# Layer A of a two-layer trunk: convolution statistics kept in PSUM, four gates kept on chip, a staging pool of its own, and x transposed eight tiles at a time

## The chip, the cores and the metric

The kernel runs on one core of one Trainium2 chip, in one launch. The metric is the device time of that launch in microseconds (us): 1713.63 us before the change, the median of three runs (1712.63 to 1716.33). Five engines work beside each other, each with its own queue in program order: PE (TensorE, matrix products), DVE (VectorE), ACT (ScalarE), POOL (GpSimd) and SP (SyncE, which issues the transfers). Instructions of different engines wait for each other by semaphores.

## The reference

Two layers over a sequence of 1024 tokens with 1024 channels, in float32. Each has one wide input projection, a token mixer, a cross-attention of four heads into 256 memory tokens, a SiLU gate over the whole branch and an output projection; the result is layer-normalized with the residual. In layer A the mixer is a convolution module over 1536 channels:

```python
def conformer_conv(u, conv_w, conv_b, g, b):
    a, gl = jnp.split(u, 2, axis=-1)
    h = a * jax.nn.sigmoid(gl)
    ...                                  # causal depthwise convolution, 31 taps
    return jax.nn.silu(layer_norm(h, g, b))

for i in range(DEPTH):                   # DEPTH = 2: layer A, layer B
    if i % 2 == 0:
        u, qm, gate = split_cols(x @ a_w_in, A_SIZES)
        y_mix = conformer_conv(u, ...)
    else:
        q, k, v, qi, ki, wi, qm, gate = split_cols(x @ b_w_in, B_SIZES)
        y_mix = dsa_attention(...)       # top-256 keys per query, ALiBi
    y_mem = mem_cross_attention(qm, layer_norm(mem), w_mkv)
    y = concatenate([y_mix, y_mem]) * silu(gate)
    x = layer_norm(ALPHA * x + y @ w_out, pg, pb)
```

## The kernel before

**Numbers.** Every fp32 operand of a product is split into a rounded high part and the rest (`hi`, `lo`), and a product is three matmuls (L149, L151, L153 in the input projections; L585, L586, L587 in the output projection). `split_w` loads a piece of weights into `wr`, of which there are three buffers; ScalarE writes the high part `wh` (L131) and POOL the low part `wl` (L132), with six buffers each. So a weight piece can be split when the piece six before it has been used. Activations lie with channels on the partitions, in eight blocks of 128 by 1024 tokens (`xhi`, `xlo`).

**Stages of layer A.** x is loaded and transposed. Twelve blocks of convolution channels follow in pairs, on TensorE as products with the input weights and on VectorE as 31 taps (L433). The sums over channels are gathered on POOL in `sumd` and `sumsq`. Channels 0 to 7 are stored to memory (`d_dram`), channels 8 to 11 stay in the four `co` buffers. Between them stand the four heads of the memory attention (`head_a`) and the twelve gates (`gate_a`: product, SiLU at L325, store to `gate_dram`). Between the gates 2 to 9 stand the keys and values of the memory attention of layer B (`k_b`, `v_b`, called K0, V0 and so on here): eight products of 256 columns, whose result goes through the tile `kvr` (tag `mp`, one buffer, which the softmax of layer A's memory attention uses too) to memory.

**The normalization.** Two products with a matrix of ones (L524, `tot`) sum over the partitions. The mean and 1/std are then written to `sumd` and `sumsq` in SBUF (L530 to L534).

**The output projection.** 16 row blocks of `a_w_out` in four groups of four: first 12 to 15 (memory heads, in `yhi`, `ylo`), then 8 to 11 and 0 to 3 (in `xhi`, `xlo`), then 4 to 7 (again in `yhi`, `ylo`). A group has two column halves with eight token blocks each, so 16 PSUM tiles of twelve matmuls. `WO12.0` is row block 12, column half 0. VectorE adds each tile to `accA` in SBUF, which begins as x (L590, L592). Beside it `conv_y` makes the operand for the next groups: load `dr` (L606), subtract the mean (L611), multiply by 1/std (L612), SiLU on ScalarE (L613), multiply by the gate (L614), split on ScalarE and POOL (L172, L173). After the last group each token block is normalized, transposed four tiles at a time and split for layer B.

**PSUM.** There are eight banks of 128x512. `ps1` holds two for products (`pj`) and two for transposes and scores (`pt`). `psb` has two tiles of two banks (x transposes, two convolution accumulators, `tot`); after the sums are done, `pso` takes its four banks for the output projection.

**Order.** The program is written in the order of the stages; a scheduler with a simulated timeline then sets the order of instructions on each engine, and each engine runs its queue in that order. A pool that is closed frees its space for the next pool, once the last users of its tiles are done.

Of the kernel before, what the change touches and what calls it, by code (L numbers as in the profile page):

```python
# [20 lines left out]
P = 128  # L21
# [43 lines left out]
def trunk(ctx, tc, x, mem, mem_g, mem_b, a_w_in, conv_w, conv_b, ln_g, ln_b,  # L65
# [43 lines left out]
    def psum_t():  # L109
        p, n = banks["pt"]  # L110
        return p.tile([P, 512], F32, tag="pt", bufs=n, name=f"pt{uid()}")
# [95 lines left out]
            nc.vector.scalar_tensor_tensor(dst[:, c], dst[:, c], rs, b[:, c], op0=OP.mult, op1=OP.add)  # L207
            nc.sync.dma_start(o[:, c], dst[:, c])

    def transpose_in(src, hi, lo, t, f=None):  # L210

        for g in range(2):
            o = psum_t()
            for j in range(4):
                k = 4 * g + j
                nc.tensor.transpose(o[:, j * P:(j + 1) * P], src[:, k * P:(k + 1) * P], ident)
            dh, dl = hi[:, 4 * g:4 * g + 4, t * P:(t + 1) * P], lo[:, 4 * g:4 * g + 4, t * P:(t + 1) * P]
            split_ps(dh, dl, o.rearrange("p (a b) -> p a b", a=4))

    def dram(name):  # L220
        return tc.dram_tile([P, T], F32, name=name)

# [2 lines left out]
    with ExitStack() as actx:  # L225
# [4 lines left out]
        def co_tile(name):  # L230
            return convp.tile([P, T], F32, tag="co", bufs=4, name=name)

        hctx = ExitStack()
        hp = hctx.enter_context(pool("hp"))
        c_sh = hp.tile([P, T], F32, name="c_sh")
        psb = hctx.enter_context(pool("psb", side="right", space=PSUM))
        mctx = ExitStack()
        am = mctx.enter_context(pool("am", side="right"))

# [3 lines left out]
        def x_load(t):  # L243
            nc.sync.dma_start(xn[t], x[t * P:(t + 1) * P, :])

        def x_in(t):
            o = psb.tile([P, T], F32, tag="acc", bufs=2, name=f"px{t}")
            for k in range(KD):
                nc.tensor.transpose(o[:, k * P:(k + 1) * P], xn[t][:, k * P:(k + 1) * P], ident)
            split_ps(xhi[:, :, t * P:(t + 1) * P], xlo[:, :, t * P:(t + 1) * P], o.rearrange("p (a b) -> p a b", a=KD))  # L250

        rows = [am.tile([NR, n], F32, tag="sg", bufs=2, name=f"rows{i}") for i, n in enumerate((T, 512))]

        def rows_load():
            nc.gpsimd.memset(rows[1][32:, :], 0.0)
# [18 lines left out]
        def mem_prep():  # L274
            mn = []
            for t in range(2):
                mt = am.tile([P, T], F32, tag="sg", bufs=2, name=f"mt{t}")
# [187 lines left out]
        def head_a(h):  # L465
            kv = am.tile([P, T], F32R, tag="kv", bufs=1, name=f"kva{h}")
            y = am.tile([P, T], F32, tag="y", bufs=1, name=f"ya{h}")
            mem_k(a_w_mkv, h, kv=kv)
            sg = am.tile([P, T], F32, tag="sg", bufs=2, name=f"msgA{h}")
            silu_gate(am, a_w_in, A_GATE + CONV_CH + h * P, sg)  # L470
# [15 lines left out]
            nc.sync.dma_start(kvb_dram[h][:, :512], kr[h])  # L486

        def gate_a(i):
            sg = am.tile([P, T], F32, tag="sg", bufs=2, name=f"ga{i}")
            silu_gate(am, a_w_in, A_GATE + i * P, sg)  # L490
            nc.sync.dma_start(gate_dram[i], sg)

        def u_conv(i):
            hs = [u_pair(i, start=i == 0), u_pair(i + 1)]
# [16 lines left out]
        u_conv(10)  # L511
        gate_a(1)
        head_a(3)
        for i in range(2, 10):
            gate_a(i)
            ((k_b, v_b)[i % 2])((i - 2) // 2)

        with tc.high_priority(offset=3000):
            tot = []
            for src in (sumd, sumsq):  # L520
                o = psb.tile([P, T], F32, tag="acc", bufs=2, name=f"tot{len(tot)}")
                for hf in range(2):
                    hs = slice(hf * 512, (hf + 1) * 512)
                    nc.tensor.matmul(o[:, hs], ones, src[:, hs], start=True, stop=True)  # L524
                tot.append(o)
            mean_b, rstd_b = sumd, sumsq
            for hf in range(2):
                hs = slice(hf * 512, (hf + 1) * 512)
                sq = hp.tile([P, 512], F32, tag="sig", bufs=2, name=f"meansq{hf}")
                nc.scalar.activation(mean_b[:, hs], tot[0][:, hs], AF.Copy, scale=1.0 / CONV_CH)  # L530
                nc.scalar.activation(sq, mean_b[:, hs], AF.Square)
                nc.vector.scalar_tensor_tensor(sq, tot[1][:, hs], 1.0 / CONV_CH, sq, op0=OP.mult, op1=OP.subtract)
                nc.scalar.activation(rstd_b[:, hs], sq, AF.Sqrt, bias=eps)
                nc.vector.reciprocal(rstd_b[:, hs], rstd_b[:, hs])  # L534
        hctx.close()
        yy = actx.enter_context(pool("yy"))
        yhi = yy.tile([P, 4, T], F32R, name="yhi")
# [12 lines left out]
            (sub or nc.vector).tensor_tensor(dl, raw, dh.bitcast(F32), op=OP.subtract)  # L550

        for h in range(MEM_HEADS):
            load_y(am, "sg", ymem_dram[h], yhi[:, h, :], ylo[:, h, :])
            if h % 2 == 1:
                gate_a(10 + h // 2)
        mctx.close()

        if "A1" in dbg:
            for i in range(NCONV):
# [3 lines left out]
            return  # L563


        octx = ExitStack()
        banks["pj"] = (octx.enter_context(pool("pso", side="right", space=PSUM)), 4)
        ao = octx.enter_context(pool("ao", side="right"))
        acc = [ao.tile([P, T], F32, name=f"accA{t}") for t in range(NB)]

        def out_group(w_out, k0, yh, yl, acc, t_order, first=False, after=None, resident=None):

            held, cur = {}, None
            for (hf, t) in t_order:
                if hf != cur:
                    cur = hf
                    if resident is None or hf not in held:
                        held[hf] = [split_w(w_out[(k0 + k) * P:(k0 + k + 1) * P, hf * 512:(hf + 1) * 512], [P, 512],
                                            resident and resident(hf, k)) for k in range(4)]
                    wts = held[hf]  # L580
                o = psum()
                tsl = slice(t * P, (t + 1) * P)
                for k in range(4):
# [19 lines left out]
        def conv_y(i, dh, dl):  # L603
# [2 lines left out]
                nc.sync.dma_start(d, d_dram[i])  # L606
            else:
                d = conv_out[i]
            gt = ao.tile([P, T], F32, tag="gt", bufs=3, name=f"gt{i}")
            nc.sync.dma_start(gt, gate_dram[i])  # L610
            nc.vector.tensor_tensor(d, d, mean_b, op=OP.subtract)  # L611
            nc.vector.tensor_tensor(d, d, rstd_b, op=OP.mult)  # L612
            nc.scalar.activation(d, d, AF.Silu, bias=chan[:, i, TAPS + 2:TAPS + 3], scale=chan[:, i, TAPS + 1:TAPS + 2])  # L613
# [18 lines left out]
        def finish_a(t, hf):  # L632
# [6 lines left out]
            transpose_in(z, xhi, xlo, t)  # L639
            if "A2" in dbg:  # L640
                nc.sync.dma_start(out[t * P:(t + 1) * P, :], z)

        def keep_a(hf, k):
# [2 lines left out]
                g = ao.tile([P, T], F32R, tag="gt", bufs=3, name=f"wg{n}")  # L646
                return g[:, :512], g[:, 512:]

            def own_place(n):
                return [ao.tile([P, 512], F32R, name=f"w{q}{n}") for q in "hl"]  # L650
            return None if hf == 0 else (own_place if k < 2 else gate_place)

        out_group(a_w_out, ids[0], yh, yl, acc, token_major, after=finish_a, resident=keep_a)
        octx.close()
        banks["pj"] = (ps1, 2)
    if "A2" in dbg:
        return

# [443 lines left out]
    with ExitStack() as octx:  # L1102
# [27 lines left out]
        for gi, k0 in enumerate((12, 0, 4, 8)):  # L1130
# [3 lines left out]
                for j in range(4):  # L1134
                    load_y(bo, "yraw", yb_d[k0 + j], yh[:, j, :], yl[:, j, :], gate_d[k0 + j] if k0 + j in LATE_GATES else None)
            if gi < 3:
                out_group(b_w_out, k0, yh, yl, acc, half_major, first=gi == 0)
            else:
                out_group(b_w_out, k0, yh, yl, acc, token_major, after=finish_b, resident=lambda hf, k: keep_b)


# [26 lines left out]
```

## Time and profile before

| | |
|---|---|
| time, median of 3 runs | 1713.63 us (1712.63 to 1716.33) |
| profiled execution | 1715.64 us, span 1713.6 us |
| mean granted TensorE clock | 0.991 |
| PE busy | 1651.4 us, 96% |
| DVE, ACT, POOL busy | 68%, 44%, 41% |
| layer A | to about 800 us |
| keys and values of layer B, gates 3 to 9 | about 470 to 585 us |
| output projection of layer A | 604 to 800 us, groups from 604, 649, 700 and 751 |

The span runs from the first to the last instruction of the profiled execution; the time of the execution has some 2 us around it. An engine's busy time counts its instructions' durations once where they overlap. In the rows below a time in square brackets is what the engine stood idle before the instruction, with the instruction that released it. Matmuls overlap: a product of 512 columns is listed with 0.39 us, and the next one starts 0.23 us after it.

### The profile page before, as it was taken

To read this page: it belongs to the slowest core of one execution; us is meant where nothing else is said; L and a number is where in the kernel's file an instruction comes from. 1 tells how busy PE (TensorE), PEld (TensorE's weight loads), DVE (VectorE), ACT (ScalarE), POOL (GpSimd) and SP (SyncE) were. 2 spreads that over 40 slices of the span, in tenths; PEclk is the share of its full clock that TensorE was granted. 3 is DMA by queue.
4 is the path that set the end of the run, shared out by engine and by line. 5 is a ranking of instruction groups with operands and counts; after the bars stand their busy time and mean duration, and the time that the engine had idled before them with its cause. 6 is when DMAs were issued, how large, how long until landed. Compare 5 with 4: busy or idle time off the path is not lost.

```text
span 1713.6 us, 22459 instructions
## 1 busy us (share of the span) xinstructions
PE 1651.4 (96%) x8214; PEld 1381.1 (81%) x8214; DVE 1173.3 (68%) x1800; ACT 753.3 (44%) x1412; POOL 694.7 (41%) x591
## 2 busy tenths in 40 slices
PE   7999999999999997999999999799999999999997
PEld 6877888888888876788767877688898888888886
DVE  3799899989996649447158999865555554535337
ACT  4333344444443524124456776354544544543221
POOL 2344554645556346444222332433323332342233
PEclk9999999999999999999999999999999999999999
DMA  5121212222243475123221333212121221246212
GB/s 183 50 58 66 86 53 84 68 68 74 74 130 116 131 282 177 62 81 114 62 65 39 92 93 98 86 38 81 50 64 55 74 68 50 63 149 250 86 44 98
DMA packets 138941, 156.88 MB, mean 92 GB/s; under 512 B 8074, under 2 KB 108426, under 8 KB 138832
## 3 DMA queue, kind: packets, MB, share of 16 engines
q1 hardware_dynamic: 138832, 155.47, 28.4%
q8 instruction: 64, 1.05, 0.3%
q14 instruction: 45, 0.37, 0.1%
HBM read 114.81 MB, written 38.80 MB: 90 GB/s over the span
## 4 chain that ended last, share of the span: by engine, by line
PE 57%; DVE 14%; ACT 4%; issue 3%; DMA 2%; POOL 1%; SPq 0%; DVEq 0%; ACTq 0%; POOLq 0%
PE pj L149 9%; PE pj L151 9%; PE pj L153 9%; PE pj L587 5%; PE pj L585 5%; PE pj L586 5%; DVE junk L829 4%; PE pt L981 2%; DVE xs L788 2%; PE S L951 1%; ACT junka L835 1%; PE S L953 1%; PE S L952 1%; PE pv L993 1%; PE pv L997 1%
## 5 line engine op out<-in xcount | busy, mean ns | idle before, releaser
L149 PE MATMUL pj<-xhi,wh 128*128 128x512 f32 (+2 forms) x1328 | 523.9, 395 | 19.1 <-ACT gB L706 10.8
L132 POOL TENSOR_TENSOR wl<-wr,wh 128x512 fp32r<-128x512 f32 (+1 forms) x260 | 352.5, 1362 | 433.7 <-ACT wh L131 412.6
L151 PE MATMUL pj<-xlo,wh 128*128 128x512 f32 (+2 forms) x1328 | 521.6, 393 | 0.6 <-DVE xlo L169 0.5
L153 PE MATMUL pj<-xhi,wl 128*128 128x512 f32 (+2 forms) x1328 | 522.1, 393 | 0.0
L433 DVE SCALAR_TENSOR_TENSOR acc<-h,chan,acc 128x996 f32<-128x996 f32 (+27 forms) x348 | 418.7, 1265 | 16.1 <-ACT acc L423 14.8
L149 PEld LDWEIGHTS pj<-xhi,wh 128*128 128x128 f32 (+1 forms) x1328 | 250.9, 189 | 73.0 <-ACT gB L706 11.6
L153 PEld LDWEIGHTS pj<-xhi,wl 128*128 128x128 f32 (+1 forms) x1328 | 251.1, 189 | 49.6 <-issue 0.2
L151 PEld LDWEIGHTS pj<-xlo,wh 128*128 128x128 f32 (+1 forms) x1328 | 251.1, 189 | 48.9 <-DVE xlo L169 1.4
L131 ACT ACTIVATE wh<-wr 128x512 fp32r<-128x512 f32 x232 | 144.6, 628 | 296.3 <-PE pj L151 155.2
L585 PE MATMUL pj<-wh,xhi 128*128 128x512 f32 x384 | 149.2, 395 | 11.2 <-DVE accA L592 7.7
L586 PE MATMUL pj<-wl,xhi 128*128 128x512 f32 x384 | 150.0, 393 | 0.0
L587 PE MATMUL pj<-wh,xlo 128*128 128x512 f32 x384 | 148.5, 393 | 0.0
L961 POOL TENSOR_SCALAR t<-t,smB 128x128 f32<-128x128 f32 (+3 forms) x96 | 71.6, 747 | 183.1 <-DVE smB L960 87.5
L956 DVE CUSTOM_DVE_ANT_0 t<-S,xs 128x128 f32<-128x128 f32 (+3 forms) x96 | 70.9, 756 | 72.7 <-PE S L953 49.8
L169 DVE TENSOR_TENSOR pl<-pt,ph 128x512 fp32r<-128x512 f32 (+1 forms) x120 | 69.2, 580 | 59.4 <-ACT ph L168 58.5
L585 PEld LDWEIGHTS pj<-wh,xhi 128*128 128x128 f32 x384 | 72.8, 190 | 29.2 <-DVE accA L592 8.6
L959 ACT ACTIVATE t<-t,mxB 128x128 f32<-128x128 f32 (+3 forms) x96 | 74.1, 774 | 46.3 <-DVE mxB L958 46.0
L168 ACT ACTIVATE ph<-pt 128x512 fp32r<-128x512 f32 (+1 forms) x120 | 60.2, 509 | 77.1 <-PE pt L981 71.1
L835 ACT ACTIVATE junka<-xs,cand 128x896 bf16<-128x896 f32 (+2 forms) x93 | 80.3, 864 | 28.3 <-DVE cand L860 22.9
L829 DVE TENSOR_SCALAR_CACHE_REDUCE junk<-xs,cand 128x1024 bf16<-128x1024 f32 (+2 forms) x93 | 89.9, 967 | 2.2
L587 PEld LDWEIGHTS pj<-wh,xlo 128*128 128x128 f32 x384 | 72.7, 189 | 15.7
L586 PEld LDWEIGHTS pj<-wl,xhi 128*128 128x128 f32 x384 | 72.8, 190 | 15.5
(273 smaller groups left out, 2721.0 us busy)
## 6 DMA issues: line engine op xcount, KB each, us to landing
wr<-in_a_w_in_dram SPq DMA_DIRECT2D x88, 256.0 KB
wr<-in_b_w_in_dram SPq DMA_DIRECT2D x76, 256.0 KB
wr<-in_a_w_out_dram SPq DMA_DIRECT2D x32, 256.0 KB
wr<-in_b_w_out_dram SPq DMA_DIRECT2D x32, 256.0 KB
yraw<-yb SPq DMA_DIRECT2D x16, 512.0 KB
gb<-gB SPq DMA_DIRECT2D x15, 512.0 KB
ga<-ga SPq DMA_DIRECT2D x12, 512.0 KB
gt<-ga SPq DMA_DIRECT2D x12, 512.0 KB
```

The source lines that it names most:

```text
L131: nc.scalar.activation(hi, raw, AF.Copy)
L132: nc.gpsimd.tensor_tensor(lo, raw, hi.bitcast(F32), op=OP.subtract)
L149: nc.tensor.matmul(o, wh, xh, start=(k == 0), stop=False)
L151: nc.tensor.matmul(o, wh, xl, start=False, stop=False)
L153: nc.tensor.matmul(o, wl, xh, start=False, stop=(k == KD - 1))
L433: nc.vector.scalar_tensor_tensor(dst[:, s:], h[:, :T - s], w, acc[:, s:], op0=OP.mult, op1=OP.add)
L585: nc.tensor.matmul(o, yh[:, k, tsl], wh, start=(k == 0), stop=False)
L586: nc.tensor.matmul(o, yh[:, k, tsl], wl, start=False, stop=False)
L587: nc.tensor.matmul(o, yl[:, k, tsl], wh, start=False, stop=(k == 3))
L829: nc.vector.tensor_scalar(j[:, :nk(b)], xs(b), th[:, i:i + 1], None, op0=op, op1=OP.add, accum_out=c[:, i:i + 1])
L835: nc.scalar.activation(j[:, :nk(b)], xs(b), AF.Sign, bias=th[:, i:i + 1], scale=-(2.0 ** 24), accum_out=c[:, i:i + 1])
L959: nc.scalar.activation(t, t, AF.Exp, bias=mx[:, e:e + 1], scale=s, accum_out=sm[:, e:e + 1])
```

## The change

1. *Statistics.* The mean and 1/std stay in the PSUM tiles `tot0` and `tot1`; the square root is taken into an SBUF tile half by half, with the reciprocal written to PSUM. The operations of `conv_y` that use them read one operand from PSUM.
2. *Gates.* Gates 8 to 11 aren't stored and loaded again: 8 and 9 lie in `gt` buffers, 10 and 11 in `sumd` and `sumsq`, which are free by then.
3. *Staging pool.* The tag `sg` (gates, rows, memory outputs) moves from `am` into a pool `sgp` of its own. `am` is then closed after V3, with all four K/V pairs placed at gates 2 to 5, and the pool `ao` with `accA` and `gt` is opened there.
4. *Output projection.* Its PSUM tiles alternate between the `pt` and `pj` banks of `ps1`; `psb` stays open. The x1 transposes write eight tiles into one two-bank tile of `psb`, with one split in place of two. The weights kept for the last group lie in `sg` buffers instead of tiles of their own.

```diff
-        psb = hctx.enter_context(pool("psb", side="right", space=PSUM))
+        pctx = ExitStack()
+        psb = pctx.enter_context(pool("psb", side="right", space=PSUM))
...
+        def transpose_in(src, t):
+            o = psb.tile([P, T], F32, tag="acc", bufs=2, name=f"px{uid()}")
+            for k in range(KD):
+                nc.tensor.transpose(o[:, k * P:(k + 1) * P], src[:, k * P:(k + 1) * P], ident)
+            split_ps(xhi[:, :, t * P:(t + 1) * P], xlo[:, :, t * P:(t + 1) * P], o.rearrange("p (a b) -> p a b", a=KD))
...
+        gate_here = {}
+        def gate_stay(i, g):
+            silu_gate(sgp, a_w_in, A_GATE + i * P, g)
+            gate_here[i] = g
...
-        for i in range(2, 10):
+        for i in range(2, 6):
             gate_a(i)
-            ((k_b, v_b)[i % 2])((i - 2) // 2)
+            k_b(i - 2)
+            v_b(i - 2)
+        mctx.close()
+        octx = ExitStack()
+        ao = octx.enter_context(pool("ao", side="right"))
+        acc = [ao.tile([P, T], F32, name=f"accA{t}") for t in range(NB)]
+        for i in range(6, 8):
+            gate_a(i)
...
-            mean_b, rstd_b = sumd, sumsq
+            mean_b, rstd_b = tot
...
-                nc.scalar.activation(rstd_b[:, hs], sq, AF.Sqrt, bias=eps)
-                nc.vector.reciprocal(rstd_b[:, hs], rstd_b[:, hs])
+                nc.scalar.activation(sq, sq, AF.Sqrt, bias=eps)
+                nc.vector.reciprocal(rstd_b[:, hs], sq)
...
-            load_y(am, "sg", ymem_dram[h], yhi[:, h, :], ylo[:, h, :])
+            load_y(sgp, "sg", ymem_dram[h], yhi[:, h, :], ylo[:, h, :])
             if h % 2 == 1:
-                gate_a(10 + h // 2)
-        mctx.close()
+                i = 8 + h // 2
+                gate_stay(i, ao.tile([P, T], F32, tag="gt", bufs=3, name=f"gt{i}"))
+        gate_stay(10, sumd)
+        gate_stay(11, sumsq)
...
-        octx = ExitStack()
-        banks["pj"] = (octx.enter_context(pool("pso", side="right", space=PSUM)), 4)
-        ao = octx.enter_context(pool("ao", side="right"))
-        acc = [ao.tile([P, T], F32, name=f"accA{t}") for t in range(NB)]
+        turn = [0]
+        def psum_a():
+            turn[0] += 1
+            return (psum_t if turn[0] % 2 else psum)()
...
-                o = psum()
+                o = bank()          # bank=psum_a in layer A, bank=psum in layer B
...
-            gt = ao.tile([P, T], F32, tag="gt", bufs=3, name=f"gt{i}")
-            nc.sync.dma_start(gt, gate_dram[i])
+            gt = gate_here.get(i)
+            if gt is None:
+                gt = ao.tile([P, T], F32, tag="gt", bufs=3, name=f"gt{i}")
+                nc.sync.dma_start(gt, gate_dram[i])
...
-            def own_place(n):
-                return [ao.tile([P, 512], F32R, name=f"w{q}{n}") for q in "hl"]
+            def spare_place(n):
+                g = sgp.tile([P, T], F32R, tag="sg", bufs=2, name=f"ws{n}")
+                return g[:, :512], g[:, 512:]
```

The lines of the changed kernel shift by the edit: L325 becomes L321, L359 becomes L355, L606 becomes L620, L600 becomes L614, L543 becomes L553.

How the instructions move shows at three places. First ScalarE's queue at gates 3 and 4. Before: `ga_3946` is gate 3, `wh_4125` and `wh_4131` are the weights of K1, `wh_4164` and `wh_4170` those of gate 5, `vt_4049` is V0, `mp` the softmax of the last head.

```order
L325 ACTIVATE ga_3946<-pj_3959 128x512
L131 ACTIVATE wh_4125<-wr_4123 128x512
L131 ACTIVATE wh_4131<-wr_4129 128x512
L325 ACTIVATE ga_3946<-pj_3985 128x512
L359 ACT_TABLE_LOAD
L359 ACTIVATE mp_3786,sm_3788<-pt_3789,mx_3787 128x256 x2
L131 ACTIVATE wh_4164<-wr_4162 128x512
L131 ACTIVATE wh_4170<-wr_4168 128x512
L310 ACTIVATE vt_4049<-pj_4024 128x256
L359 ACTIVATE mp_3786,sm_3788<-pt_3790,mx_3787 128x256 x2
```

Now: `ga_3993` is gate 3, `wh_4106` the second weight piece of V1, `wh_4145` and `wh_4151` are the weights of gate 4.

```order
L131 ACTIVATE wh_4106<-wr_4104 128x512
L321 ACTIVATE ga_3993<-pj_4006 128x512
L355 ACT_TABLE_LOAD
L355 ACTIVATE mp_3789,sm_3791<-pt_3792,mx_3790 128x256 x2
L131 ACTIVATE wh_4145<-wr_4143 128x512
L131 ACTIVATE wh_4151<-wr_4149 128x512
L355 ACTIVATE mp_3789,sm_3791<-pt_3793,mx_3790 128x256 x2
L321 ACT_TABLE_LOAD
L321 ACTIVATE ga_3993<-pj_4032 128x512
```

Both halves of gate 3 stood ahead of the first table load (L359); now its second half (`pj_4032`) stands behind two exponentials, the weights of gate 4, two more exponentials and a second table load.

Second SP's queue around the loads of x. Before, to the fifth of the loads: `ga_126` is the store of gate 11, `wr_5201` is `WO8.0`.

```order
L491 DMA ga_126<-ga_4808 128x1024
L122 DMA wr_5201<-in_a_w_out_dram 128x512
L600 DMA accA_4881<-in_x_dram 128x1024
L600 DMA accA_4882<-in_x_dram 128x1024
L600 DMA accA_4883<-in_x_dram 128x1024
L600 DMA accA_4884<-in_x_dram 128x1024
L600 DMA accA_4885<-in_x_dram 128x1024
```

Now, to the third of the loads: `wr_4696` is the second half of the weights of gate 9, `wr_4754` the first half of gate 10, `kvb_133` the store of K3 and V3.

```order
L122 DMA wr_4696<-in_a_w_in_dram 128x4x128
L122 DMA wr_4754<-in_a_w_in_dram 128x4x128
L482 DMA kvb_133<-kvr_4357 128x512
L614 DMA accA_4444<-in_x_dram 128x1024
L614 DMA accA_4445<-in_x_dram 128x1024
L614 DMA accA_4446<-in_x_dram 128x1024
```

All eight loads follow one another as before, but now directly behind the store of V3 and ahead of the second half of the weights of gate 10, in front of all of `a_w_out`.

Third POOL's queue where the second weight group begins. Before: `wl_5216` and `wl_5222` are `WO10.0` and `WO11.0`, `wl_5340` is `WO8.1`, `xlo<-dr` are channels 0, 1 and 2.

```order
L173 TENSOR_TENSOR xlo<-co_3435,xhi 128x1024
L173 TENSOR_TENSOR xlo<-dr_5473,xhi 128x1024
L132 TENSOR_TENSOR wl_5216<-wr_5213,wh_5215 128x512
L132 TENSOR_TENSOR wl_5222<-wr_5219,wh_5221 128x512
L132 TENSOR_TENSOR wl_5340<-wr_5337,wh_5339 128x512
L173 TENSOR_TENSOR xlo<-dr_5483,xhi 128x1024
L173 TENSOR_TENSOR xlo<-dr_5493,xhi 128x1024
```

Now: `dr_5488` is channel 3, `dr_5770` and `dr_5780` are channels 4 and 5, `wl_5201` and `wl_5207` are `WO10.0` and `WO11.0`.

```order
L173 TENSOR_TENSOR xlo<-dr_5488,xhi 128x1024
L173 TENSOR_TENSOR ylo<-dr_5770,yhi 128x1024
L132 TENSOR_TENSOR wl_5201<-wr_5198,wh_5200 128x512
L173 TENSOR_TENSOR ylo<-dr_5780,yhi 128x1024
L132 TENSOR_TENSOR wl_5207<-wr_5204,wh_5206 128x512
L173 TENSOR_TENSOR ylo<-dr_5790,yhi 128x1024
```

The low halves of `WO10.0` and `WO11.0` stood behind channel 0's split; now channels 1 to 4 stand ahead of the one and channel 5 ahead of the other. ScalarE's queue has the same sequence there: `yhi` of channel 4, `WO10.0`, `yhi` of channel 5, `WO11.0`.

## Rows read from the trace of the kernel before

**Rows 1.** The page's shares: busy us (share of the span) x instructions.
```profile
PE 1651.4 (96%) x8214; PEld 1381.1 (81%) x8214; DVE 1173.3 (68%) x1800; ACT 753.3 (44%) x1412; POOL 694.7 (41%) x591
```

**Rows 2.** Stretches of the output projection: from:to length, busy us (instructions), clock, DMA, GB/s.
```profile
604.00:649.30 45.30, 44.08 (x190) 35.42 (x190) 25.32 (x23) 10.07 (x14) 21.97 (x10) 1.00 0.74 267
649.30:700.30 51.00, 40.02 (x159) 31.32 (x158) 47.08 (x36) 21.14 (x23) 38.99 (x16) 0.93 0.46 155
```

**Rows 3.** TensorE's timeline: start, us, instruction, [idle before <- what ended it].
```profile
615.66 0.51 PE L585 MATMUL pj<-wh,yhi 128*128 128x512 f32 x1 [1.22 <-DVE accA L590]
...
653.17 0.49 PE L585 MATMUL pj<-wh,xhi 128*128 128x512 f32 x1 [2.41 <-ACT wh L131]
...
654.37 0.79 PE L585 MATMUL pj<-wh,xhi 128*128 128x512 f32 x1 [0.71 <-DVE accA L590]
...
671.02 0.79 PE L585 MATMUL pj<-wh,xhi 128*128 128x512 f32 x1 [5.33 <-DVE accA L592]
...
689.30 0.50 PE L585 MATMUL pj<-wh,xhi 128*128 128x512 f32 x1 [2.41 <-DVE accA L592]
```

**Rows 4.** Stretches behind the two longest stops of TensorE.
```profile
653.80:657.20 3.40, 2.83 (x7) 2.15 (x7) 3.40 (x3) 1.62 (x4) 3.40 (x2) 0.51 0.13 47
670.90:674.30 3.40, 3.28 (x8) 2.61 (x9) 3.40 (x4) 0.80 (x1) 2.94 (x2) 0.50 0.61 209
```

**Rows 5.** VectorE's timeline in the first two groups.
```profile
614.92 0.69 DVE L590 SCALAR_TENSOR_TENSOR accA<-accA,pj 128x512 f32<-128x512 f32 x1 [9.51 <-DMA accA<-in_x_dram]
...
622.96 0.69 DVE L590 SCALAR_TENSOR_TENSOR accA<-accA,pj 128x512 f32<-128x512 f32 x1 [1.08 <-DMA accA<-in_x_dram]
...
626.73 3.68 DVE L614 TENSOR_TENSOR co<-co,gt 128x1024 f32<-128x1024 f32 x2 [1.70 <-DMA gt<-ga]
...
641.10 1.87 DVE L611 TENSOR_TENSOR dr<-dr,sumd 128x1024 f32<-128x1024 f32 x1 [3.29 <-DMA dr<-d_dram]
...
642.89 0.67 DVE L590 SCALAR_TENSOR_TENSOR accA<-accA,pj 128x512 f32<-128x512 f32 x1
...
643.49 2.82 DVE L612 TENSOR_TENSOR dr<-dr,sumsq 128x1024 f32<-128x1024 f32 x1
...
649.10 1.21 DVE L612 TENSOR_TENSOR dr<-dr,sumsq 128x1024 f32<-128x1024 f32 x1
...
694.41 1.89 DVE L592 TENSOR_TENSOR accA<-pj,accA 128x512 f32<-128x512 f32 x3
```

**Rows 6.** SP's timeline, issues of x and of gates.
```profile
611.47 3.80 SPq L600 DMA_DIRECT2D accA<-in_x_dram  x8
615.37 13.14 SPq L610 DMA_DIRECT2D gt<-ga  x4
```

**Rows 7.** POOL's timeline: one 128x1024 operation alone, weight pieces, one split.
```profile
546.91 2.40 POOL L446 TENSOR_TENSOR co<-co,c_sh 128x1024 f32<-128x1024 f32 x1
...
605.67 2.55 POOL L132 TENSOR_TENSOR wl<-wr,wh 128x512 fp32r<-128x512 f32 x2 [5.99 <-PE pj L587]
...
641.85 3.38 POOL L173 TENSOR_TENSOR xlo<-co,xhi 128x1024 fp32r<-128x1024 f32 x1
```

**Rows 8.** ScalarE's timeline at gate 3, and one split of a channel.
```profile
485.15 0.63 ACT L131 ACTIVATE wh<-wr 128x512 fp32r<-128x512 f32 x1 [2.09 <-PE pj L151]
...
485.69 0.58 ACT L325 ACTIVATE ga<-pj 128x512 f32<-128x512 f32 x1
...
486.29 1.28 ACT L359 ACT_TABLE_LOAD   x1
...
487.58 0.47 ACT L359 ACTIVATE mp<-pt,mx 128x256 f32<-128x256 f32 x1
...
651.55 1.04 ACT L172 ACTIVATE xhi<-dr 128x1024 fp32r<-128x1024 f32 x1
```

**Rows 9.** Waits of TensorE from 485 to 500: total, times, longest.
```profile
PE pj L149 <- ACT ga L325: 1.0, 2, 0.8
PE pj L149 <- ACT vt L310: 0.9, 1, 0.9
```

More of the change, by code (lines that the diff above doesn't have):

```diff
@@ L208, in layer_norm_late @@
             nc.sync.dma_start(o[:, c], dst[:, c])
[L210 to L218, printed above, removed]
     def dram(name):
@@ L231, in co_tile @@
             return convp.tile([P, T], F32, tag="co", bufs=4, name=name)
+        sgp = actx.enter_context(pool("sgp"))
         hctx = ExitStack()
@@ L244, in x_load @@
             nc.sync.dma_start(xn[t], x[t * P:(t + 1) * P, :])
-        def x_in(t):
[L247 to L252, printed above, removed]
+        def transpose_in(src, t):
[3 more added lines that the diff above has]
+            split_ps(xhi[:, :, t * P:(t + 1) * P], xlo[:, :, t * P:(t + 1) * P], o.rearrange("p (a b) -> p a b", a=KD))
+        def x_in(t):
+            transpose_in(xn[t], t)
+        rows = [sgp.tile([NR, n], F32, tag="sg", bufs=2, name=f"rows{i}") for i, n in enumerate((T, 512))]
         def rows_load():
@@ L276, in mem_prep @@
             for t in range(2):
-                mt = am.tile([P, T], F32, tag="sg", bufs=2, name=f"mt{t}")
+                mt = sgp.tile([P, T], F32, tag="sg", bufs=2, name=f"mt{t}")
                 nc.sync.dma_start(mt, mem[t * P:(t + 1) * P, :])
@@ L468, in head_a @@
             mem_k(a_w_mkv, h, kv=kv)
-            sg = am.tile([P, T], F32, tag="sg", bufs=2, name=f"msgA{h}")
-            silu_gate(am, a_w_in, A_GATE + CONV_CH + h * P, sg)
+            sg = sgp.tile([P, T], F32, tag="sg", bufs=2, name=f"msgA{h}")
+            silu_gate(sgp, a_w_in, A_GATE + CONV_CH + h * P, sg)
             mem_v(a_w_mkv, h, kv=kv)
@@ L488, in gate_a @@
         def gate_a(i):
-            sg = am.tile([P, T], F32, tag="sg", bufs=2, name=f"ga{i}")
-            silu_gate(am, a_w_in, A_GATE + i * P, sg)
+            sg = sgp.tile([P, T], F32, tag="sg", bufs=2, name=f"ga{i}")
+            silu_gate(sgp, a_w_in, A_GATE + i * P, sg)
             nc.sync.dma_start(gate_dram[i], sg)
+        gate_here = {}
+        def gate_stay(i, g):
+            silu_gate(sgp, a_w_in, A_GATE + i * P, g)
+            gate_here[i] = g
         def u_conv(i):
@@ L563, in trunk, with out_group @@
             return
-        octx = ExitStack()
-        banks["pj"] = (octx.enter_context(pool("pso", side="right", space=PSUM)), 4)
-        ao = octx.enter_context(pool("ao", side="right"))
-        acc = [ao.tile([P, T], F32, name=f"accA{t}") for t in range(NB)]
-        def out_group(w_out, k0, yh, yl, acc, t_order, first=False, after=None, resident=None):
+        turn = [0]
+        def psum_a():
+            turn[0] += 1
+            return (psum_t if turn[0] % 2 else psum)()
+        def out_group(w_out, k0, yh, yl, acc, t_order, first=False, after=None, resident=None, bank=psum_a):
             held, cur = {}, None
@@ L638, in finish_a @@
             nc.sync.dma_start(x1_dram[t], z)
-            transpose_in(z, xhi, xlo, t)
+            transpose_in(z, t)
             if "A2" in dbg:
@@ L647, in gate_place @@
                 return g[:, :512], g[:, 512:]
-            def own_place(n):
-                return [ao.tile([P, 512], F32R, name=f"w{q}{n}") for q in "hl"]
-            return None if hf == 0 else (own_place if k < 2 else gate_place)
+            def spare_place(n):
+                g = sgp.tile([P, T], F32R, tag="sg", bufs=2, name=f"ws{n}")
+                return g[:, :512], g[:, 512:]
+            return None if hf == 0 else (spare_place if k < 2 else gate_place)
         out_group(a_w_out, ids[0], yh, yl, acc, token_major, after=finish_a, resident=keep_a)
         octx.close()
-        banks["pj"] = (ps1, 2)
+        pctx.close()
     if "A2" in dbg:
@@ L1136, in trunk @@
             if gi < 3:
-                out_group(b_w_out, k0, yh, yl, acc, half_major, first=gi == 0)
+                out_group(b_w_out, k0, yh, yl, acc, half_major, first=gi == 0, bank=psum)
             else:
-                out_group(b_w_out, k0, yh, yl, acc, token_major, after=finish_b, resident=lambda hf, k: keep_b)
+                out_group(b_w_out, k0, yh, yl, acc, token_major, after=finish_b, resident=lambda hf, k: keep_b, bank=psum)
 _INS = ["x", "mem", "mem_ln_g", "mem_ln_b", "a_w_in", "a_conv_w", "a_conv_b", "a_ln_g", "a_ln_b", "a_w_mkv", "a_w_out",
```

## The prediction, made before the changed kernel had run

> **What bounds the kernel now.** I read the engines' shares first. TensorE is busy for 96% of the span [rows 1], so time comes only from holes in its stream, or from stretches at the lower clock. The products are the same before and after; the question is which holes go and which come. All of the change lies in layer A, which ends near 800 us. Layer B is left out below, since its instructions and their order stay as they are.
>
> The table by stage comes next. In the output projection of layer A the first weight group (604 to 649) is nearly full: 190 matmuls in 44.1 us, a step of 0.23 us. The second group has TensorE busy for 40.0 us of 51.0, VectorE for 47.1, and a mean clock of 0.93 [rows 2]. So the holes are there, and VectorE is the engine that is short.
>
> The matmul rows with a bracket give the holes one by one, with what ended them [rows 3]: 1.22 us at 615.66, 2.41 and 0.71 at 653.17 and 654.37, 5.33 at 671.02, 2.41 at 689.30, together 12.1 us. All but the first at 653 wait for an eviction (L590, L592) on VectorE. Behind the second and the third place the granted clock is 0.5, the 1.2 GHz level, for 3.4 us [rows 4]; the engine had idled for 2.41 and 0.71 us, and for 5.33, before it fell. Of these stretches 2.83 and 3.28 us are busy at half rate, so half of that is lost: 3.0 us. Sum of what can be won: 15.1 us.
>
> Why VectorE is late stands in its own rows [rows 5]. The first eviction waited 9.51 us for `accA`, the rows of x, which are issued only at 611.47 behind weights on SP's queue: 4 MB, with four gates of 2 MB behind them [rows 6]. The gates of channels 8 to 11 are multiplied in only at 626.73. So the other eight channels (`dr`, three operations each) begin at 641.10 and fill the queue to 694, between the evictions of the second group.
>
> **The change, part by part.** *x early, gates on chip.* Eight loads of x move on SP from behind `WO8.0` to ahead of the second half of gate 10's weights, about 60 us earlier; four gate stores and four gate loads go. No eviction waits for x then, and channels 8 to 11 are finished when gate 11 is. The `dr` loads, which need the buffers of channels 8 to 11, come some 30 us earlier, counted from the start of the projection, and the `dr` work lies beside the first group. All holes above hang on the late queue: −15.1 us. x ahead of gate weights costs nothing by my count: 11.5 us pass from its first issue to the eviction of its sixth tile [rows 5, 6], and gate 10's second half is used an estimated 25 us after its issue in the new order.
>
> *New waits in the first group.* `dr` now competes with the evictions from 8 us on, with two to five of its operations between two evictions. An operation with two SBUF inputs takes 1.21 alone (649.10) and 2.82 (643.49) beside a POOL subtraction that runs from 641.85 for 3.38 us; an eviction, which reads PSUM, takes 0.67 in the same stretch (642.89) [rows 5, 7]. In the new code two of three `dr` operations read PSUM. I walked the new VectorE order with these: 1.21 for the operations on PSUM, 1.21 to 2.82 for the product with the gate. Tile 12 of 16 waits 0.8 us (0 to 4) for its bank. On POOL the low half of `WO15.1` now stands behind the split of channel 1 (2.40 alone; 1.28 for a weight piece, of which 605.67 shows two [rows 7]), and waits another 2.0 (0 to 4). Sum +2.8, range 0 to 6.
>
> The Trainium skill, "SBUF — State Buffer", section "Who interferes with whom", says that a VectorE instruction with at most one SBUF input doesn't contend with GpSimd and one with two does. The trace agrees: 0.67 against 2.82. Were it not so for the new operations, the second rival below would be the forecast.
>
> *A new wait at the second group.* On ScalarE the split of channel 4 into `yhi` now stands before the high half of `WO10.0`; on POOL `ylo` of channels 4 and 5 stands before the low halves of `WO10.0` and `WO11.0`. The first group reads `yhi` of that channel until nine steps, 2.1 us, before its end. From there ScalarE needs 1.04 [rows 8] and POOL 2.40 + 1.28 + 2.40 + 1.28 = 7.4, so `WO11.0` is ready 6.3 us after the group's end. TensorE wants it ten steps, 2.3 us, after that end. Idle: 4.0 us in two pieces, 1.2 and 2.8, with the semaphores 4.2. Such a pair lowered the clock before, which cost 1.5; I take half: 0.8. Sum +5.0, range 0 to 7. What goes at 653 comes back by another wait.
>
> *Keys and values of layer B together.* Four K/V blocks move between gates 2 to 6. The copy of K0 out of PSUM needs the buffer of the softmax tile `mp`, so its bank is taken until `mp` is transposed; V0, both halves of gate 3 and K1 go through the one other bank. K1 waits for the eviction of gate 3's second half. Before that stand on ScalarE: the second weight piece of gate 4 (0.63; it can't start until that half of gate 3 ends), two exponentials (0.47 each), a table load (1.28), and the eviction itself (0.58) [rows 8], 3.4 us with the semaphores. By the same kind of step V0's bank is late for gate 3 by 1.1, K0's bank for V1 by 1.5, and the copy before V1's transposes by 0.8. Sum 6.8. Against it the waits of this stretch now, 1.0 and 0.9 [rows 9], go: net +4.9, range 2 to 6. For a fall of the clock behind 3.4 and 1.5 us, half of 1.5: +0.8 (0 to 1.5).
>
> *Statistics in PSUM.* One switch more from SiLU to Sqrt and back, two table loads. They stand between the evictions of gates 8 and 9, whose banks are wanted some 4 us later; with that cover gone they cost 2.6. Channels 8 to 11 are normalized some 3 us sooner. I take 0.
>
> The Trainium skill, "ScalarE: Activation LUTs", speaks against this edit: by the section "Table sets: the hidden batching unit" calls are to be batched by set, and "What ACT_TABLE_LOAD costs" has 1.28 us for the load and 1.38 for a drain. The trace shows the first and not the second: the load starts 0.02 us after the SiLU's end, the exponential 0.01 after the load's [rows 8]. By the page's figure, as an estimate, K1's wait would be 1.4 longer and the time 1713.4.
>
> *Output banks and transposes.* Four PSUM banks alternate as four did. The x1 transposes become one eviction of 1024 elements for two of 512, with slack in the order behind the last matmul of each block: 0, from −1 to +2.
>
> **The sum.** −15.1 + 2.8 + 5.0 + 4.9 + 0.8 = −1.6. The profiled execution took 1715.6 us with a span of 1713.6, and becomes 1714.0. The median of the three runs, 1713.6, is 2.0 below it; on that scale the time is 1712.0 us. 0.2%, about 3.4 us, is what a measurement of this kernel tells from no change.
>
> **The rivals.** *Most of the gain stays.* If POOL and VectorE run ahead of my walk, the 2.8 and 5.0 don't arise: −15.1 + 4.9 + 0.8 = −9.4, 1704. For it: VectorE is busy for only 25.3 of 45.3 us in the first group now [rows 2]. Against it: the orders on ScalarE and POOL are fixed, and `yhi` can't be written sooner.
>
> *VectorE becomes the bound of the first group (slower).* It needed 53 us for the `dr` work with its evictions, 641 to 694 [rows 5]. If it needs as many now, the queue starts 8 us into a group of 45 and ends 16 us behind it, and the waits for evictions (1.22 + 0.71 + 5.33 + 2.41 = 9.7, with the clock's 3.0: 12.7) return in another place: −15.1 + 12.7 + 5.0 + 4.9 + 0.8 = +8.3, 1722. It decides if a `dr` operation takes over 2 us on average. For it: the product with the gate keeps two SBUF inputs. Against it: two thirds of the operations read PSUM.
>
> *x comes late all the same.* Its loads need the space of the memory attention's tiles, and SP waits in order. If that comes free at 575 and not at 555, the weights of gates 10 and 11 come behind 11.5 us of transfers: some +3, 1715 to 1717. Against it: the last of these tiles is stored with V3, before gate 7.
>
> **How the numbers follow.** Forecast 0.45 (1708 to 1716), gain stays 0.27 (1699 to 1708), VectorE's queue 0.18 (1716 to 1727), x late 0.10. Range 1702 to 1719. Faster by over 0.2%, below 1710.2: the second case and a third of the forecast's, 0.42. Slower, above 1717.0: 0.20. Between: 0.38.
>
> **What would show it.** Right: no wait for `accA<-in_x_dram`; some 3.4 us of idle before K1's first matmul, released by the gate's SiLU on ScalarE; at the start of the second group two waits on POOL's weight pieces, 4 us together; full rate from there on. Wrong: VectorE busy for over 0.9 of the first group, with `dr` operations of 3 us (second rival); no wait at K1, its bank having come free another way; holes before gates 10 and 11 (third); any difference in layer B.

## The result, and the profile after

The changed kernel takes 1703.98 us, the median of four runs (1702.78 to 1705.93), against 1714.29 in four runs of the kernel before. The ratio is 0.994, with a 95% interval of 0.9923 to 0.9958: 10.3 us faster. The forecast was 1712.0, between 1702 and 1719. The side and the range held; the size did not, since 1.6 us were expected.

TensorE's busy time fell by 4.7 us, some 3 of them from the two stretches of the projection that no longer run at half rate, and VectorE's by 25 us ([rows 1] and the page of the kernel before). The page's shares after:

```profile
PE 1646.7 (97%) x8214; PEld 1379.7 (81%) x8214; DVE 1148.6 (68%) x1792; ACT 755.8 (44%) x1406; POOL 681.0 (40%) x591
```

Three stretches of the changed kernel, in the columns of [rows 2]. The first is the place of the K/V blocks, the other two are the first weight group of the output projection, shifted by some 4 us, and the second.

```profile
488.00:496.00 8.00, 4.64 (x36) 4.14 (x35) 8.00 (x10) 4.68 (x9) 4.42 (x7) 1.00 0.38 131
607.70:652.27 44.57, 43.29 (x187) 34.79 (x186) 40.16 (x40) 20.64 (x23) 28.97 (x13) 1.00 0.59 189
652.27:695.80 43.53, 43.53 (x194) 36.03 (x192) 11.26 (x17) 9.28 (x15) 21.01 (x13) 1.00 0.22 73
```

The first group has VectorE at 40.2 us of 44.6 and POOL at 29.0, where they had 25.3 and 22.0; the second has TensorE without a hole, and VectorE at 11.3 of 43.5 where it had 47.1 of 51.0. The work of the `dr` channels has moved by a group, and VectorE is busy for 0.90 of the first group. The clock is 1.00 throughout, so both falls of [rows 4] are gone.

The second stretch of [rows 2] stops inside the second group of the kernel before: VectorE adds the group's sixteenth tile only at 708.24, so the third group begins near 708 and not at 700. What can be set side by side is the second and third group together, from the first matmul on `xhi` to the first of the last group, which is on `yhi` again. Before:

```profile
649.23 0.39 PE L585 MATMUL pj<-wh,xhi 128*128 128x512 f32 x1
...
751.56 0.40 PE L585 MATMUL pj<-wh,yhi 128*128 128x512 f32 x1
```

In the changed kernel the last group begins with this row, and the second with one at 652.27 (shown further below):

```profile
739.32 0.40 PE L599 MATMUL pt<-wh,yhi 128*128 128x512 f32 x1
```

The two groups took 102.3 us and take 87.1.

The waits that are left between 465 and 800 us, as rows of TensorE's timeline (a fourth, of 0.7, stands before V1's transposes, and a fifth, of 0.24, before gate 3 at 476.69, for V0's bank):

```profile
492.29 0.39 PE L149 MATMUL pj<-mhi,wh 128*128 128x256 f32 x1 [3.36 <-ACT ga L321]
...
497.62 0.39 PE L149 MATMUL pj<-mhi,wh 128*128 128x256 f32 x1 [1.34 <-ACT kvr L298]
...
640.99 0.50 PE L599 MATMUL pt<-wh,yhi 128*128 128x512 f32 x1 [1.28 <-DVE accA L604]
```

Two of the three are the new ones before K1 and V1, the third a bank in the first group; the five of [rows 3] are gone. ScalarE's rows before the first of them answer to [rows 8]: a weight piece, an exponential, the table load, and then the eviction for which K1 waited.

```profile
488.79 0.63 ACT L131 ACTIVATE wh<-wr 128x512 fp32r<-128x512 f32 x1 [2.14 <-PE pj L151]
...
489.32 0.46 ACT L355 ACTIVATE mp<-pt,mx 128x256 f32<-128x256 f32 x1
...
490.34 1.28 ACT L321 ACT_TABLE_LOAD   x1
...
491.64 0.60 ACT L321 ACTIVATE ga<-pj 128x512 f32<-128x512 f32 x1
```

SP's rows, to set against [rows 6]: x is issued at 545 in place of 611, and `dr` begins at 610 in place of 636.

```profile
545.28 4.86 SPq L614 DMA_DIRECT2D accA<-in_x_dram  x8
...
609.66 6.03 SPq L620 DMA_DIRECT2D dr<-d_dram  x3
```

### The profile page after: what moved, and what is told of

It reads as the page before. It is cut to its first block, busy times and chain, and to the rows that moved or that the text cites. A ratio compares the mean times of both kernels' runs of the same rounds, so it can differ in the third digit from the quotient of the medians.

```text
span 1700.0 us, 22441 instructions
## 1 busy us (share of the span) xinstructions
PE 1646.7 (97%) x8214; PEld 1379.7 (81%) x8214; DVE 1148.6 (68%) x1792; ACT 755.8 (44%) x1406; POOL 681.0 (40%) x591
## 4 chain that ended last, share of the span: by engine, by line
PE 53%; DVE 12%; ACT 3%; issue 2%; POOL 1%; DMA 0%; DVEq 0%; ACTq 0%; POOLq 0%
PE pj L149 7%; PE pj L151 7%; PE pj L153 7%; PE pj L601 5%; PE pj L599 5%; PE pj L600 5%; DVE junk L846 3%; PE pt L998 2%; DVE xs L805 2%; PE pt L599 1%; PE pt L601 1%; PE pt L600 1%; PE S L968 1%; PE S L970 1%; PE S L969 1%
## 5 line engine op out<-in xcount | busy, mean ns | idle before, releaser
L132 POOL TENSOR_TENSOR wl<-wr,wh 128x512 fp32r<-128x512 f32 x258 | 340.3, 1325 | 436.8 <-ACT wh L131 416.5
L429 DVE SCALAR_TENSOR_TENSOR acc<-h,chan,acc 128x996 f32<-128x996 f32 (+27 forms) x348 | 418.5, 1263 | 16.4 <-ACT acc L419 15.1
L131 ACT ACTIVATE wh<-wr 128x512 fp32r<-128x512 f32 (+1 forms) x230 | 143.9, 629 | 309.8 <-PE pj L151 153.7
L600 PE MATMUL pj<-wl,xhi 128*128 128x512 f32 x320 | 124.1, 390 | 0.0
L599 PE MATMUL pj<-wh,xhi 128*128 128x512 f32 x320 | 123.3, 390 | 0.0
L601 PE MATMUL pj<-wh,xlo 128*128 128x512 f32 x320 | 122.6, 390 | 0.0
L600 PEld LDWEIGHTS pj<-wl,xhi 128*128 128x128 f32 x320 | 60.1, 188 | 12.9
L601 PEld LDWEIGHTS pj<-wh,xlo 128*128 128x128 f32 x320 | 60.0, 188 | 12.9
L599 PEld LDWEIGHTS pj<-wh,xhi 128*128 128x128 f32 x320 | 60.1, 188 | 12.8
```

Of the source, the lines that this page charges most:

```text
L131: nc.scalar.activation(hi, raw, AF.Copy)
L132: nc.gpsimd.tensor_tensor(lo, raw, hi.bitcast(F32), op=OP.subtract)
L429: nc.vector.scalar_tensor_tensor(dst[:, s:], h[:, :T - s], w, acc[:, s:], op0=OP.mult, op1=OP.add)
```

## The experiments

The theory to test: the holes went since VectorE's queue starts early, for which x, the gates and the statistics each have a part, and the K/V blocks give some of it back. The rivals: x alone did it; the gates' transfers alone; the PSUM operands alone. Times are set beside 1714.7 to 1714.9 us of the kernel before, and the ratio is to that kernel.

**Statistics back in SBUF.** First the base for it, the gates stored and loaded again in their old places:

```diff
-        for i in range(6, 8):
+        for i in range(6, 10):
             gate_a(i)
...
-                i = 8 + h // 2
-                gate_stay(i, ao.tile([P, T], F32, tag="gt", bufs=3, name=f"gt{i}"))
-        gate_stay(10, sumd)
-        gate_stay(11, sumsq)
+                gate_a(10 + h // 2)
```

> The changed kernel, but gates 8 to 11 made, stored and loaded in the places they had before the change (8 and 9 ahead of the sums, 10 and 11 between the loads of the memory heads), so that the two staging buffers aren't wanted by the memory heads first, as they were in e3_gates_dram. If the gates' way through memory matters by itself: channels 8 to 11 get their product some 10 us after gate 11, 2 to 6 us of waits in the projection, 1706 to 1710 us. If only the buffers mattered in e3_gates_dram: 1704 to 1705 us.

Measured: 1710.5 us, ratio 0.9975 (0.9965 to 0.9986), 6.5 us over the changed kernel. The waits of TensorE from 600 to 700 and two rows of VectorE:

```profile
PE pt L596 <- DVE accA L601: 3.8, 2, 3.3
PE pj L596 <- ACT ga L321: 1.3, 1, 1.3
PE pj L596 <- DVE accA L601: 1.2, 1, 1.2
```

```profile
610.94 2.82 DVE L627 TENSOR_TENSOR co<-co,gt 128x1024 f32<-128x1024 f32 x1 [2.15 <-DMA gt<-ga]
...
624.50 1.23 DVE L627 TENSOR_TENSOR co<-co,gt 128x1024 f32<-128x1024 f32 x1 [2.13 <-DMA gt<-ga]
```

Channels 10 and 11 got their gates at 610.9 and 624.5, after waits for the loads; in the changed kernel the last was multiplied at 610.6. 6.3 us of waits stand in the first group, for 1.3 in the changed kernel. The gates on chip, with the places that they have in the changed kernel, are worth 6.5 us: the first case of the expectation, 0.5 over its range. 5.0 of it stand in the trace as waits; the twelve runs of this kernel lie between 1705.6 and 1716.4. Then, on top of that kernel:

```diff
-            mean_b, rstd_b = tot
+            mean_b, rstd_b = sumd, sumsq
```

> The kernel of e6_gates_as_before, with mean and 1/std in SBUF as before the change. Theory S (operations with two SBUF inputs wait for POOL, those with one in PSUM don't): dr operations of 2 to 3.4 us beside POOL, late evictions, 8 to 12 us over e6_gates_as_before. Rival (e4_stats_sbuf was slow by its other order after the 9 us hole): within 2 us of e6_gates_as_before.

Measured: 1717.8 us, ratio 1.0018 (1.0009 to 1.0027), 7.3 us over the kernel above, a little under the 8 to 12 of theory S and far from the rival's 2. The three `dr` operations by line on VectorE, from 600 to 680 (busy us, mean ns of one, idle before), here:

```profile
L627 DVE TENSOR_TENSOR dr<-dr,gt 128x1024 f32<-128x1024 f32 x8 | 14.1, 1760 | 1.4 <-ACT dr L626 1.4
L624 DVE TENSOR_TENSOR dr<-dr,sumd 128x1024 f32<-128x1024 f32 x8 | 15.0, 1880 | 2.9 <-DMA dr<-d_dram 2.9
L625 DVE TENSOR_TENSOR dr<-dr,sumsq 128x1024 f32<-128x1024 f32 x8 | 16.1, 2022 | 0.0
```

and in the changed kernel, from 596 to 670:

```profile
L630 DVE TENSOR_TENSOR dr<-dr,gt 128x1024 f32<-128x1024 f32 x8 | 11.6, 1454 | 0.0
L627 DVE TENSOR_TENSOR dr<-dr,tot 128x1024 f32<-128x1024 f32 x8 | 9.7, 1210 | 2.1 <-DMA dr<-d_dram 2.1
L628 DVE TENSOR_TENSOR dr<-dr,tot 128x1024 f32<-128x1024 f32 x8 | 9.7, 1209 | 0.0
```

Subtraction and product with 1/std took 1.88 and 2.02 us each with SBUF operands, and 1.21 in all sixteen cases with one in PSUM; the product with the gate keeps two SBUF inputs in both, and is slowed in both. A pair of rows shows how, POOL's first, then VectorE's:

```profile
640.15 3.39 POOL L173 TENSOR_TENSOR xlo<-dr,xhi 128x1024 fp32r<-128x1024 f32 x1
...
641.20 3.43 DVE L625 TENSOR_TENSOR dr<-dr,sumsq 128x1024 f32<-128x1024 f32 x1
```

POOL's split ran from 640.15 to 643.54; VectorE's product was issued at 641.20 and ended at 644.63, 1.09 us behind it, with its own 1.21 us nearly all after POOL's end. Evictions had to wait behind such operations:

```profile
PE pt L596 <- DVE accA L601: 9.8, 2, 6.1
```

The same edit on a worse base says it again. This is the base, with the gates through memory and staging buffers that the memory heads want first:

```diff
             if h % 2 == 1:
-                i = 8 + h // 2
-                gate_stay(i, ao.tile([P, T], F32, tag="gt", bufs=3, name=f"gt{i}"))
-        gate_stay(10, sumd)
-        gate_stay(11, sumsq)
+                gate_a(8 + h // 2)
+        gate_a(10)
+        gate_a(11)
```

> The changed kernel, but gates 8 to 11 are stored to memory and loaded again, as before. Theory (the gain is VectorE's queue starting early, for which both x and the gates must be there): the products of channels 8 to 11 wait for their gates at the start of the projection, dr follows later, waits of 2 to 5 us come back: 1706 to 1709 us. Rival G (the transfers of the gates were the whole of it): 1712 to 1715. Rival X (only the early x matters): 1704, no holes in the projection beyond the one of 1.3 us.

> The kernel of e3_gates_dram, with mean and 1/std written to SBUF as before the change. Theory: within 2 us of e3_gates_dram, since VectorE has slack in the first group once it starts early. Rival S (the operations that read PSUM don't contend with POOL, and that is what makes VectorE keep up): dr operations take 2 to 3.4 us, evictions late, 5 to 10 us over e3_gates_dram.

Measured: 1715.7 us, ratio 1.0005 (0.9996 to 1.0014), and with the statistics in SBUF 1726.7, ratio 1.0072 (1.0059 to 1.0085): 11 us more. Both theories missed. That of the second expectation (within 2 us) fell, and its rival S held, at 11 for 5 to 10. The first kernel's time, far over the 1706 to 1709 of its theory, looks like rival G, but its trace tells of another cause. The projection has no hole at all; one wait of 10.9 us stands at 574, where gate 8 and the memory heads want the same two staging buffers:

```profile
PE pj L149 <- ACT ga L321: 14.3, 2, 10.9
```

```profile
579.86 4.63 ACT L628 ACTIVATE co<-co,chan 128x1024 f32<-128x1024 f32 x4 [1.49 <-DVE co L627]
584.40 1.07 ACT L321 ACTIVATE ga<-pj 128x512 f32<-128x512 f32 x2
```

ScalarE's gate eviction started at 584.40. Two things end there: the first of VectorE's two subtractions for `ylo` (from 583.13, 2.35 together), which lets a staging buffer go, and the four SiLUs of the `co` channels that stood before it on ScalarE. Which of them held it isn't shown; both stood behind VectorE's reciprocals and products of the `co` channels. So that kernel did not measure the gates' way through memory; the one with the old places did.

**x late.**

```diff
         for t in range(NB):
+            nc.gpsimd.tensor_copy(acc[t][:, 0:1], sumsq[:, T - 1:T])
             nc.sync.dma_start(acc[t], x[t * P:(t + 1) * P, :])
```

> The changed kernel, with a one-column copy on POOL from the tile of gate 11 into each tile of x ahead of its load, so that x is loaded after gate 11, as late as before the change; the column is overwritten by the load. Rival X (the gain is x being there early): the first evictions wait for x by 5 to 10 us, dr follows later, holes in the first two groups come back: 1710 to 1715 us. Theory S (the statistics in PSUM and the gates on chip let VectorE catch up): one hole of 1 to 3 us in the first group, none in the second: 1705 to 1707 us.

Measured: 1710.5 us, ratio 0.9976 (0.9967 to 0.9985), 6.5 us over the changed kernel. The time is at the lower end of the rival's range; the pattern is that of theory S with a larger hole, one in the first group and none in the second. SP's issue of x, VectorE's first eviction, and TensorE's only wait in the projection over 0.3 us:

```profile
615.92 5.36 SPq L615 DMA_DIRECT2D accA<-in_x_dram  x8
...
622.12 0.69 DVE L604 SCALAR_TENSOR_TENSOR accA<-accA,pt 128x512 f32<-128x512 f32 x1
```

```profile
PE pt L599 <- DVE accA L604: 6.6, 1, 6.6
```

x was issued at 615.9, behind three `dr` loads, and the first eviction came at 622.1. After that VectorE caught up by itself: the second group has no hole. In the kernel before, late x and late gates had moved the `dr` work into the second group; with the other two edits in place, late x costs its own wait and the half clock behind it, no more.

**The K/V blocks.** Their new place alone, in the kernel before:

```diff
-        for i in range(2, 10):
+        for i in range(2, 6):
             gate_a(i)
-            ((k_b, v_b)[i % 2])((i - 2) // 2)
+            k_b(i - 2)
+            v_b(i - 2)
+        for i in range(6, 10):
+            gate_a(i)
```

> The kernel before with one edit: the four K/V pairs of layer B stand together at gates 2 to 5, gates 6 to 9 follow. Theory (the new place of K/V costs 3.7 us by itself, 5.6 of waits for 1.9): 1717 to 1719 us, ratio 1.002, with a wait of some 3.4 us before K1. Rival (the place is harmless, the wait before K1 comes from the other edits): 1714 us, ratio 1.000.

Measured: 1717.5 us, ratio 1.0016 (1.0007 to 1.0025), 2.8 us slower, with the waits of the theory:

```profile
PE pj L149 <- ACT ga L325: 3.4, 1, 3.4
PE pj L149 <- ACT kvr L302: 1.3, 1, 1.3
PE pt L313 <- ACT vt L310: 0.7, 1, 0.7
```

The rival is out: these waits come with the place. The cause was to be the one buffer of `mp`:

```diff
-            kr[h] = am.tile([P, 512], F32, tag="mp", bufs=1, name=f"kvr{h}")
+            kr[h] = am.tile([P, 512], F32, tag="kvr", bufs=2, name=f"kvr{h}")
```

> The changed kernel with one edit: the tile kvr gets a tag of its own with two buffers, in place of the one buffer of mp. Theory (K0's PSUM bank is held because its copy needs the buffer of the softmax tile): the waits of 3.4 us before K1 and 1.3 us before V1 go or shrink to under 1 us each, time 1700 to 1701 us, ratio to the kernel before 0.992. Rival (ScalarE's queue sets the wait, with its table loads and weight pieces, whichever bank is free): the same waits under other names, 1704 us, ratio 0.994.

Measured: 1701.1 us, ratio 0.992 (0.9907 to 0.9933), 2.9 us faster than the changed kernel. In the place of the K/V blocks one wait is left, which is later and smaller:

```profile
PE pj L149 <- ACT ga L321: 2.7, 1, 2.7
```

```profile
493.69 0.38 ACT L298 ACTIVATE kvr<-pj 128x256 f32<-128x256 f32 x1
...
501.56 1.28 ACT L321 ACT_TABLE_LOAD   x1
...
502.85 0.60 ACT L321 ACTIVATE ga<-pj 128x512 f32<-128x512 f32 x1
```

The waits before K1 and V1 are gone, and the two smaller ones with them, so the bank was what held K1 and V1. The new one stands at gate 4, whose second half uses the bank of its first, since the other bank still holds V1, copied at 511.17 only. The eviction of the first half is at 502.85 behind a table load at 501.56, and the load behind the last exponentials' split. The rival holds for this rest. It says how to go on: put the K/V blocks one gate later, so that the exponentials are over before K1.

```diff
         # kvr with buffers of its own, as above
-        for i in range(2, 6):
+        gate_a(2)
+        for i in range(3, 7):
             gate_a(i)
-            k_b(i - 2)
-            v_b(i - 2)
+            k_b(i - 3)
+            v_b(i - 3)
...
-        for i in range(6, 8):
-            gate_a(i)
+        gate_a(7)
```

> The changed kernel with kvr in buffers of its own, as in e1_own_kvr, and the four K/V pairs one gate later, at gates 3 to 6, so that the last exponentials of the memory attention are over before K1 needs a bank. If the 2.7 us left in e1_own_kvr come from table loads and exponentials ahead of a gate's eviction, they go: 1697 to 1699 us. If the later loads of x (they wait for V3) cost as much: 1701 us.

Measured: 1695.9 us (1694.5 to 1696.5), ratio 0.9891 (0.9878 to 0.9903): 8 us faster than the changed kernel and 19 faster than the one before, a little under the range expected. All waits of TensorE from 465 to 830 us in it:

```profile
PE pt L599 <- DVE accA L604: 0.7, 1, 0.7
PE pj L149 <- DVE kl L169: 0.2, 1, 0.2
```

This version beats both kernels. Of the 5.2 us to the kernel above it 2.7 are the wait that went; the rest isn't explained, and the spans of the two profiled executions (1697.6 and 1694.1) differ by 3.5.

## Why the prediction was right and wrong

*The holes of the projection, −15.1.* Right. All five went, with both falls of the clock; the second and third group, where four of them stood, are 15.3 us shorter, for 13.9 in the sum (10.9 in those four and 3.0 of clock). The account of what does it was too short: it named x and the gates. The runs give three edits about the same size, 6.5 us for x, 6.5 for the gates, 7.3 for the statistics (the last on top of the gates). They don't add up. A kernel with early x, but gates and statistics as before, has a ratio of 1.0018, and the kernel before with the K/V blocks moved 1.0016: early x, with the new pools and output banks that this comparison holds too, gave nothing by itself. The queue on VectorE has to be both early and quick. The gates and the PSUM operands were not put alone into the kernel before.

*Statistics in PSUM, 0.* Wrong as a term, though its effect was in the walk: I took 1.21 us for operations that read PSUM, and the 16 rows show 1.21. The pair of rows behind this reading, 0.67 against 2.82, set an operation of 512 columns beside one of 1024; the fair pair is 1.21 against 1.88 to 2.02. The second rival, VectorE as the bound of the first group, is what happens without this edit: its condition was a mean over 2 us, and at 1.76 to 2.02 there were already 9.8 us of waits. With the edit it was near: VectorE is busy for 0.90 of the first group, the share named as a sign of it, but with `dr` operations of 1.21 to 1.45 us on average in place of 3.

*New waits in the first group, +2.8.* The bank of a tile in the second half cost 1.28 for 0.8 expected. The 2.0 for `WO15.1` on POOL did not come.

*A new wait at the second group, +5.0.* This is the step that failed. ScalarE and POOL did what the step said, and later by 1.4 us (`WO11.0` 7.7 after the group's start for 6.3): POOL's rows at the start of the second group (652.27) are the two splits and the two weight pieces.

```profile
652.36 2.77 POOL L173 TENSOR_TENSOR ylo<-dr,yhi 128x1024 fp32r<-128x1024 f32 x1 [9.78 <-ACT yhi L172]
655.08 1.30 POOL L132 TENSOR_TENSOR wl<-wr,wh 128x512 fp32r<-128x512 f32 x1
656.34 2.39 POOL L173 TENSOR_TENSOR ylo<-dr,yhi 128x1024 fp32r<-128x1024 f32 x1
658.69 1.29 POOL L132 TENSOR_TENSOR wl<-wr,wh 128x512 fp32r<-128x512 f32 x1
```

`WO10.0` was ready at 656.38 and `WO11.0` at 659.98. I had let TensorE take the twelve matmuls of a tile in a row, and want them 1.6 and 2.3 us (seven and ten steps) after 652.27. Its rows tell otherwise:

```profile
652.27 0.39 PE L599 MATMUL pt<-wh,xhi 128*128 128x512 f32 x1
...
656.13 0.39 PE L601 MATMUL pt<-wh,xlo 128*128 128x512 f32 x1
...
656.36 0.39 PE L599 MATMUL pt<-wh,xhi 128*128 128x512 f32 x1
...
658.62 0.39 PE L600 MATMUL pt<-wl,xhi 128*128 128x512 f32 x1
...
661.34 0.39 PE L600 MATMUL pt<-wl,xhi 128*128 128x512 f32 x1
```

The queue opens tiles in four banks and takes the two first row blocks of three of them, 18 matmuls to 656.13, before the first matmul with `WO10.0` (its high half, 656.36). The low half is first used at 658.62, that of `WO11.0` at 661.34, 2.2 and 1.4 us after they were ready. The new order on TensorE was there to be read; I had read it for ScalarE, POOL and VectorE alone. The half of a clock fall that hung on this wait went with it.

*K/V together, +4.9.* Right in its mechanism and in three of four sizes: 3.36 for 3.4 before K1, 1.34 for 1.5 before V1, 0.7 for 0.8 at the transposes. Of the 1.1 between V0 and gate 3 only 0.24 came. 5.6 for 1.9 is +3.7. The clock stayed at its upper level after 3.36 us of idle (the row of 488 to 496), so in this execution the +0.8 fell away too. That was luck: four kernels of the experiments fell to half behind the same wait (last section), and there V1 came 6.7 to 7.9 us after K1, for 5.3 here.

*Output banks and transposes, 0.* No run takes them back. From the first matmul of the last group to the same matmul of layer B (820.27 before, 807.59 now) it is 68.3 us for 68.7, so nothing speaks against the 0.

*The sum by what was measured.* −15.1 + 1.3 + 3.7 = −10.1; the medians differ by 10.3. So close a match is partly chance: each median is of four runs that spread over 3 us or more, and the spans of the two profiled executions differ by 13.6, of which 11.8 lie between the last convolution products and layer B (15.3 won in the second and third group, 4.0 lost ahead of them, 0.4 won behind) and the rest in stretches that the change was not to touch. Of the rivals the first, "most of the gain stays", at 1704, is what happened, by its number and not by its reason: it had POOL ahead of my walk, and POOL was 1.4 us behind it. I gave it 0.27, since I thought the orders on ScalarE and POOL decided. The table loads cost nothing where they were added; a load and an eviction took 1.28 and 0.60 with 0.02 us between, as before, and no drain showed between them. x came at 545, not at 575, so the third rival is out.

## What to carry to other kernels

When a wait is added on a feeding engine, read the consumer's new order too: an order that opens several accumulations can put first what is ready early, and here the last late piece was used at 661.34, some 6.8 us later than a tile-by-tile order would have wanted it. An operand that is used many times beside a busy GpSimd is better left in PSUM, where these operations took 1.21 us in place of 1.9 to 2.0. And before a bank is thought to be short, look at which buffer its eviction needs: one tile with a tag of its own, and a place one gate later, gave 8 us on top of the change.

## What the runs showed of the hardware that was not expected

The same idle of 3.36 us before K1 had the granted clock at 1.00 in three profiles (the changed kernel, x late, the statistics in SBUF) and at 0.50 to 0.56 for the next 3.4 us in four (the K/V blocks moved alone, the gates back in their old places, and both kernels with the worse base). The gates in their old places, to set against the row of 488 to 496:

```profile
489.80:493.20 3.40, 3.37 (x15) 3.37 (x16) 3.40 (x4) 0.56 (x1) 1.54 (x4) 0.50 0.58 214
```

Other places: half after an idle of 6.6 us (x late, 622.8 to 626.2 at 0.52) and, in the kernel with the statistics in SBUF, after idles of 3.67 and 6.12 us (0.50 each); with the K/V blocks moved alone, after an idle of 4.05, it was 1.00 for 0.8 us and 0.53 for the next 3.4. So in these runs idles of 3.36 to 4.05 us were followed by either level: the length of one such idle alone did not tell which, and the same wait cost a varying amount.

In the kernel with the statistics in SBUF nine rows of VectorE operations with two SBUF inputs that met a running POOL operation end 1.08 or 1.09 us after it (the pair of rows above is one of them), where such an operation alone takes 1.21: nearly as if each had waited for the whole of it.
